# A decoder step on one core: earlier transfers for the pooling buffers, a held background convolution, a separate key loop and other filler places

## The chip, the core and the metric

The kernel runs on one core of a Trainium2 chip. Its time is the device time of one execution in microseconds (us); the lower, the better. TensorE (PE in the rows) multiplies, VectorE (DVE) and ScalarE (ACT) do everything elementwise, GpSimd (POOL) and SyncE (SP) mostly issue transfers.

## What is computed

One step of a two-layer decoder trunk, over 1024 prompt positions and 8 samples of 8 positions (1088 columns in all), with 1024 features in float32. Layer 0 is a mixer of two branches, layer 1 a pooling mixer; each is followed by a SwiGLU network.

```python
def _conformer_conv(u, buf, w_dw, b_dw, g, b):          # layer 0, branch 1
    a, gate = jnp.split(u, 2, axis=-1)
    glu = a * jax.nn.sigmoid(gate)
    ext = jnp.concatenate([buf.astype(glu.dtype), glu], axis=1)
    y = lax.conv_general_dilated(ext, ...)              # 31 taps, each channel by itself
    y = y + b_dw.astype(y.dtype)
    y = jax.nn.silu(_layernorm(y, g, b))                # mean and variance over 512 channels
    return y, ext[:, -(CONV_WIDTH - 1):]
...
def _pool_mixer(xn, buf, pos0, w_pool, pool_scale):     # layer 1
    ext = jnp.concatenate([buf.astype(xn.dtype), xn], axis=1)
    ...                                                 # per group: trailing mean over 2, 4, 8 or 16, minus the token
    y = jnp.einsum('btgc,gcd->btgd', d, w_pool).reshape(n, t, D_MODEL)
    return y * pool_scale.astype(y.dtype), ext[:, -POOL_BUF:]
```

Branch 2 of layer 0 is sliding-window attention with sinks. `buf` of the pooling mixer is zero for the prompt; for the samples it is the input `state_pool` (15 earlier positions of each sample), which the kernel holds in HBM as `spool`.

## The kernel before

Features lie on the 128 partitions, positions along the columns. The 1088 columns are cut into NC = 4 chunks of TW = 272, two chunks to a half h (h = 0 and 1); the samples are the last 64 columns of chunk 3. Every float32 product is made of three matmuls of split operands (`mm3`, L311), whose high and low parts are made by `split` (L323): ScalarE writes the high part, VectorE the low one. A weight tile is transferred on SP's queue (`Weights.raw`, L127) and split in the same way (`whi`, `wlo`). The sums over channels for the norms are matmuls with a constant matrix (`ones_d`, `ones_v`, `ones_h`) in plain float32.

TensorE executes in the order of the program. On the other engines a scheduler lays down a fixed order when the kernel is built, in which a ready instruction can be put ahead of an earlier one that is not ready; each engine then executes its own list strictly in that order. Work that belongs to a matmul's result is put in `later` and written by `flush` (L300) at the end of the next `mm3` or step. The convolution's 31 taps per channel tile (`conv_taps`, L445; 480 columns for h = 1, 544 for h = 0) and the samples' convolution (`conv_sample`, L460) are background work of VectorE: they stand in `bg` (h = 0 and samples) and `bg1` (h = 1), and `pump` (L306) writes some of them whenever its estimate of VectorE's time is behind that of TensorE. `bg` goes ahead of `bg1`.

The stages that the change touches, in order of time:

- Input projection (L602 to L643). `Glu(0)` and the key weights go through one loop over the chunks: `gl.a(c)`, `gl.g(c)`, then `measure(c + 1)` (L413: squares of the next chunk, eight float32 matmuls, reciprocal root, and, by `later`, that chunk's split operands), then `heads('k', u, c)`.
- Attention (L645 to L812). 16 steps of `turn` (transposes), `scores` and `values_out`. The 16 parts of `Glu(2)` and `Glu(3)` are fillers: four go ahead of the loop, and every step i except 15 calls `filler()`, so that the twelve that are left go into steps 0 to 11. `filler` without a part only calls `flush`.
- Output projection (L873 to L909). First the four attention tiles, then the four convolution tiles; `while bg` at o == 1 empties `bg`, and `Layer(0)` (L473) makes the norm over channels: mean matmuls, `center`, variance matmuls, reciprocal root, `out`. Mean and variance are eight matmuls each.
- `half_pass` (L1093), four times: a SwiGLU network for one half, in NP = 11 stages j of `gate_up` (seven steps of 24 matmuls) and `down`. In the first one, `while bg1` and `Layer(1)` stand at j == 9. In the second and third, `pool_in` and `pool_mix` at j = 2, 4, 6 and 8 (`POOL_AT`) make one of the four pooling groups for half 0 and half 1. The samples are in half 1: for chunk 3, `pool_in` takes a tile `es` from the seven rotating buffers `t` (`wide`, L271), fills it from `spool` on POOL's queue and writes the new state out on the same queue:

```python
            if c == NC - 1:
                es = wide()[:, :DEC * (PB + DEC)].rearrange("p (b t) -> p b t", b=DEC)
                G.dma_start(out=es[:, :, 0:PB], in_=I['spool'][:, kt])
                V.scalar_tensor_tensor(es[:, :, PB:], src[:, n:]..., gain, r[:, n:]..., ALU.mult, ALU.mult)
                s, inv = sums(es, g, DEC)
                ...
                G.dma_start(out=O['pool_s'][:, kt], in_=es[:, :, DEC:])
```

  This happens twice per group (k = 0 and 1), with 60 KB each. The tile `ca1` is a single buffer, in which the taps of h = 1 and then the reciprocal root of `Layer(1)` lie.
- `emit_y` (L1075) writes the result out on SP's queue, two row tiles at a time.

Of the kernel before, what the change touches and what calls it, by code (L numbers as in the profile page):

```python
# [18 lines left out]
P = 128  # L19
# [229 lines left out]
def _body(ctx, tc, I, O):  # L249
# [21 lines left out]
    def wide():  # L271

        return tp.tile([P, PB + 2 * TW + 1], F32, tag="t", bufs=NT, name="t")

    def both():
        return pair_of(wide())
# [18 lines left out]
    def bank2():  # L295
        return pp.tile([P, 2, 512], F32, tag="pp", name="pp")[:, :, :TW]

    later, bg, bg1 = [], deque(), deque()

    def flush():  # L300
        todo, later[:] = list(later), []
        for f in todo:
            f()
        pump()

    def pump(slack=0.0):  # L306
        while (bg or bg1) and V.t < T.t + slack:
            (bg or bg1).popleft()()
        V.t = max(V.t, T.t - LAG)

# [162 lines left out]
    class Layer:  # L473
# [3 lines left out]
        def __init__(self, h):  # L477
            self.h = h
            e = [E[h][:, ct, 0:2 * TW] for ct in range(CT)]
            e2 = [pair_of(x) for x in e]  # L480
            mb = bank2()
            for ct in range(CT):
                for k in range(2):
                    T.matmul(out=mb[:, k], lhsT=ones_v, rhs=e2[ct][:, k], start=ct == 0, stop=ct == CT - 1)

            def center():
                sqs = []
                for ct in range(CT):
                    V.scalar_tensor_tensor(e2[ct], mb, 2.0, e2[ct], ALU.mult, ALU.add)
                    sq = both()  # L490
                    S.activation(sq, e2[ct], AF.Square)
                    sqs.append(sq)
                later.append(lambda: var(sqs))

            def var(sqs):
                vb = bank2()
                for ct in range(CT):
                    for k in range(2):
                        T.matmul(out=vb[:, k], lhsT=ones_v, rhs=sqs[ct][:, k], start=ct == 0, stop=ct == CT - 1)
                r = pair_of((cvp, tp)[h].tile([P, 2 * TW], F32, tag=f"ca{h}", bufs=1, name="ca"))  # L500
                rsqrt_of(r, vb, 1, lambda: out(r))

            def out(r):
                for ct in range(CT):
                    V.tensor_tensor(e2[ct], e2[ct], r, ALU.mult)
                    S.activation(e[ct], e[ct], AF.Silu, scale=pcol('cn_g', ct), bias=pcol('cn_b', ct))
            later.append(center)
# [84 lines left out]
    def heads(name, u, c):  # L592
        b = project(u, c)
        o = C0[c]
        if name == 'k':
            head_norm(b, c, [(HALF[kv], kz[HALF[kv], kv, o:o + TW]) for kv in range(2)], pcol('kg'))
        elif name == 'v':
            values(b, c)
        else:
            head_norm(b, c, [(slice(0, P), Q[c // 2][:, int(name[1]), c % 2 * TW:c % 2 * TW + TW])], pcol('qg'))  # L600
# [3 lines left out]
    for c in range(NC):  # L604
        gl.a(c)
        if c == 0:
            for kt in range(KT):
                feed(x0[0][:, kt, :], kt == 0, 0)
        gl.g(c)
        if c + 1 < NC:  # L610
            measure(c + 1)
        if c == 0:
            w0.pop(0)()
        heads('k', u, c)
    flush()
    x0_pool.__exit__(None, None, None)
# [183 lines left out]
            split(y.pair(p), Q[h][:, 2 * p:2 * p + 2, :])  # L800

    for i in range(16):
        if i != 15:
            filler()
        if i == 13:
            Y = Act(xp, 0)
            attn_split(0, Y)
        turn(i)
        if i + 2 < 16:
            scores(i + 2)  # L810
        values_out(i)
# [29 lines left out]
    def operands(h, goff):  # L841
# [28 lines left out]
                job(diff, 'T3', 'B22', 'B12', 'B12'), job(cut, 'B22', 12), job(cut, 'T3', 10), job(cut, 'T4', 14)]  # L870
        return x, deque(first), deque(rest)

    ua = W.take(4)  # L873
    for o in range(KT):
        b = bank2()
# [138 lines left out]
    def sums(e, g, n):  # L1014
# [6 lines left out]
            cur, wd = nx, 2 * wd  # L1021
        return cur, 1.0 / wd

    def pool_in(c, g):

        x = slot(xp, c % 2, 4)
        r, n = RS[c // 2][:, c % 2], PC[c]
        for k in range(2):
            kt = 2 * g + k
            gain, src = pcol('norm_mix', KT + kt), pair_of(rt(c // 2, kt))[:, c % 2]  # L1030
            e, d = ext[k], tmp()
            S.activation(e[:, 0:PB], halo[:, kt, :], AF.Copy)
            V.scalar_tensor_tensor(e[:, PB:PB + n], src[:, :n], gain, r[:, :n], ALU.mult, ALU.mult)
            S.activation(halo[:, kt, :], e[:, n:n + PB], AF.Copy)
            s, inv = wide(), 0.5 / 2 ** g
            w = 2 * 2 ** g
            if g == 0:
                V.tensor_tensor(s[:, PB:PB + n], e[:, PB:PB + n], e[:, PB - 1:PB - 1 + n], ALU.add)
            else:
                V.tensor_tensor_scan(s[:, 0:PB + n], e[:, 0:PB + n], hist[k][:, 16 - w:16 - w + PB + n], 0.0,  # L1040
                                     ALU.add, ALU.subtract)
            V.scalar_tensor_tensor(d[:, 0:n], s[:, PB:PB + n], inv, e[:, PB:PB + n], ALU.mult, ALU.subtract)
            if c == 0:
                t = hp.tile([P, 16], F32, tag="s16", bufs=2, name="s16")
                V.tensor_tensor(t, s[:, PB:PB + 16], pcol('rcnt', 16 * g, 16), ALU.mult)
                V.tensor_tensor(d[:, 0:16], t, e[:, PB:PB + 16], ALU.subtract)
            if c == NC - 1:
                es = wide()[:, :DEC * (PB + DEC)].rearrange("p (b t) -> p b t", b=DEC)
                G.dma_start(out=es[:, :, 0:PB], in_=I['spool'][:, kt])
                V.scalar_tensor_tensor(es[:, :, PB:], src[:, n:].rearrange("p (b t) -> p b t", b=DEC), gain,  # L1050
                                       r[:, n:].rearrange("p (b t) -> p b t", b=DEC), ALU.mult, ALU.mult)
                s, inv = sums(es, g, DEC)
                V.scalar_tensor_tensor(d[:, n:].rearrange("p (b t) -> p b t", b=DEC), s[:, :, PB:], inv,
                                       es[:, :, PB:], ALU.mult, ALU.subtract)
                G.dma_start(out=O['pool_s'][:, kt], in_=es[:, :, DEC:])
            split((x[:, k, :], x[:, 2 + k, :]), d)
        if c == NC - 1 and g == 3:
            G.dma_start(out=O['pool_p'], in_=halo)
        return x
# [13 lines left out]
            feed_res(half, oo)  # L1073

    def emit_y(h, o):  # L1075
        if o % 2 == 1:
            nc.sync.dma_start(out=O[f'y{h}'][:, o - 1:o + 1, :], in_=res[h][o // 4][:, o % 4 - 1:o % 4 + 1])

    POOL_AT = {2: 0, 4: 1, 6: 2, 8: 3}
# [13 lines left out]
    def half_pass(l, half, x, pooled, after, following, mixed=False):  # L1093
# [4 lines left out]
        for j in range(NP):  # L1098
            if pooled is not None and j == 1:
                finish(pooled)  # L1100
                flush()
            if pooled is not None and j in POOL_AT:
                ds = [pool_in(c, POOL_AT[j]) for c in (2 * pooled, 2 * pooled + 1)]
            if mixed and j == NP - 2:
# [30 lines left out]
            steps.popleft()()  # L1135
        return nx if following is not None else None

    plan(0, False, True)
    plan(0, True)
    plan(1, True)  # L1140
# [142 lines left out]
```

## Time and profile before

| | before |
|---|---|
| median of 3 runs | 2000.65 us (1999.78 to 2005.07) |
| the profiled execution | 2002.05 us, of which the span is 2000.3 us |
| TensorE busy | 1909.4 us, 95% of the span |
| VectorE busy | 1670.3 us, 84% |
| ScalarE busy | 946.5 us, 47% |
| granted TensorE clock, mean | 0.981 of full speed |

The profile is of one execution. The span runs from the first instruction to the last, and 1.75 us lie outside of it. Busy shares are means over stages that differ much; so the profile is read by stage, and a stage's idle time of TensorE together with its granted clock tells what could be had there. One step of matmuls with 272 columns can be seen at either of the two clock levels, and where the granted clock is 0.5 it takes twice the time.

### The profile page before, as it was taken

The numbers are of one execution on the slowest core, as the hardware profiler recorded it, in microseconds if no ns is written. First come the engines' busy times: TensorE is split into PE (matmuls) and PEld (weight loads), VectorE is DVE, ScalarE is ACT, GpSimd is POOL, SyncE is SP. The second block draws the span as 40 slices with busy tenths as digits, with TensorE's granted clock in tenths as the row PEclk, the third lists the DMA queues.
The fourth block names the chain that finished last, engine by engine and source line by source line (L and its number), as shares of the span: only waits on it lengthen the run. The fifth ranks groups of instructions, "written<-read, shape, count | busy, mean of one in ns | idle before, by whom it ended". The sixth has DMA issues, their size and how long they took to land.

```text
span 2000.3 us, 34797 instructions
## 1 busy us (share of the span) xinstructions
PE 1909.4 (95%) x14461; PEld 1854.2 (93%) x14461; DVE 1670.3 (84%) x2587; ACT 946.5 (47%) x1613; POOL 32.6 (2%) x47
## 2 busy tenths in 40 slices
PE   7999989799999999899999999899898999999999
PEld 6898658799999999799999998898898999999998
DVE  6999999998777776998898899787787898878784
ACT  7534775544343553554544446444443544343432
POOL 1100000000000000000000000000000000000000
PEclk9999999899999999999999999999998999999999
DMA  5220103132323241132322223323223323232321
GB/s 191 89 61 1 35 9 124 43 103 88 106 85 106 85 161 54 43 132 75 117 74 98 99 85 104 76 77 114 85 76 85 118 96 127 84 107 84 107 85 67
DMA packets 52191, 177.75 MB, mean 89 GB/s; under 512 B 5968, under 2 KB 10672, under 8 KB 51488
## 3 DMA queue, kind: packets, MB, share of 16 engines
q1 hardware_dynamic: 50672, 172.12, 25.7%
q0 software_dynamic: 1360, 3.40, 0.8%
q8 instruction: 113, 1.85, 0.4%
q14 instruction: 46, 0.38, 0.1%
HBM read 169.74 MB, written 6.74 MB: 88 GB/s over the span
## 4 chain that ended last, share of the span: by engine, by line
PE 78%; DVE 14%; ACT 4%; DMA 2%; issue 2%; POOL 0%; DVEq 0%; ACTq 0%; POOLq 0%
PE pp L111 68%; PE ps L111 10%; DVE x L111 3%; DVE wlo L111 2%; DVE t L111 2%; DVE res L111 2%; DVE ca L111 2%; DMA raw<-w 1%; DVE raw L111 1%; ACT whi L111 1%; DMA t<-spool 1%; ACT P L111 1%; ACT t L111 1%; DVE ss L111 1%; ACT x L111 0%
## 5 line engine op out<-in xcount | busy, mean ns | idle before, releaser
L111 PE MATMUL pp<-x,whi 128*128 128x272 f32 x5568 | 1076.1, 292 | 38.7 <-ACT t L111 26.4
L111 PEld LDWEIGHTS pp<-x,whi 128*128 128x128 f32 x5568 | 890.0, 191 | 44.2 <-ACT t L111 28.8
L111 PE MATMUL pp<-x,wlo 128*128 128x272 f32 x2784 | 813.4, 292 | 3.6 <-DVE wlo L111 3.6
L111 ACT ACTIVATE whi<-raw 128x1024 fp32r<-128x1024 f32 (+1 forms) x390 | 407.3, 1048 | 538.4 <-PE pp L111 362.2
L111 DVE TENSOR_TENSOR wlo<-raw,whi 128x1024 fp32r<-128x1024 f32 (+1 forms) x386 | 465.0, 1209 | 118.1 <-ACT whi L111 117.7
L111 PEld LDWEIGHTS pp<-x,wlo 128*128 128x128 f32 x2784 | 532.0, 191 | 4.7 <-DVE wlo L111 4.7
L111 PE MATMUL pp<-hh,whi 128*128 128x272 f32 x1408 | 408.2, 290 | 6.6 <-DVE res L111 4.3
L111 PE MATMUL pp<-hh,wlo 128*128 128x272 f32 x1408 | 407.2, 289 | 0.0
L111 PE MATMUL pp<-hl,whi 128*128 128x272 f32 x1408 | 405.5, 288 | 0.0
L111 PEld LDWEIGHTS pp<-hh,whi 128*128 128x128 f32 x1408 | 265.1, 188 | 8.5 <-DVE res L111 4.4
L111 PEld LDWEIGHTS pp<-hl,whi 128*128 128x128 f32 x1408 | 265.3, 188 | 0.0
L111 PEld LDWEIGHTS pp<-hh,wlo 128*128 128x128 f32 x1408 | 264.8, 188 | 0.0
L111 PE MATMUL ps<-x,whi 128*128 128x272 f32 x896 | 184.3, 302 | 12.9 <-ACT whi L111 7.9
L111 DVE TENSOR_TENSOR g<-pp,g 128x544 f32<-128x544 f32 x184 | 129.6, 717 | 44.9 <-PE pp L111 44.2
L111 PEld LDWEIGHTS ps<-x,whi 128*128 128x128 f32 x896 | 147.1, 194 | 21.4 <-ACT whi L111 7.9
L111 DVE TENSOR_TENSOR t<-pp,t 128x544 f32<-128x544 f32 (+1 forms) x176 | 113.8, 647 | 43.8 <-PE pp L111 40.3
L111 DVE TENSOR_TENSOR res<-pp,res 128x544 f32<-128x544 f32 (+1 forms) x200 | 135.4, 693 | 13.4 <-PE pp L111 12.8
L111 PE MATMUL ps<-x,wlo 128*128 128x272 f32 x448 | 131.8, 294 | 0.4 <-DVE wlo L111 0.4
L111 ACT ACTIVATE hh<-t 128x272 fp32r<-128x272 f32 x176 | 74.7, 426 | 107.4 <-DVE t L111 106.7
L111 ACT ACTIVATE t<-t 128x272 f32<-128x272 f32 x170 | 72.1, 427 | 92.1 <-DVE t L111 91.6
L111 DVE TENSOR_TENSOR raw<-raw 128x1024 f32<-128x1024 f32 x88 | 107.0, 1216 | 0.0
L111 ACT ACTIVATE t<-pp 128x544 f32<-128x544 f32 (+1 forms) x176 | 97.2, 553 | 15.5 <-PE pp L111 13.7
(164 smaller groups left out, 1546.8 us busy)
## 6 DMA issues: line engine op xcount, KB each, us to landing
raw<-w SPq DMA_DIRECT2D x294, 512.0 KB, 3.3
x<-x SPq DMA_DIRECT2D x16, 272.0 KB, 8.6
res<-x SPq DMA_DIRECT2D x2, 1088.0 KB, 6.3
g<-x SPq DMA_DIRECT2D x2, 1088.0 KB, 5.7
o_y<-res SPq DMA_DIRECT2D x4, 544.0 KB, 2.7
o_y<-g SPq DMA_DIRECT2D x4, 544.0 KB, 2.7
raw<-w SPq DMA_DIRECT2D x8, 256.0 KB, 4.4
P<-bias SPq DMA_DIRECT2D x2, 512.0 KB, 4.5
```

What stands on the lines that cost most here:

```text
L111: return f(*a, **k)
```

## The change

Seven edits:

1. Pooling. The samples' buffer `es` no longer comes out of `t`. A new function `history(g)` takes one tile for both k out of the single buffer `ca1` and issues both `spool` transfers on POOL's queue; it is called in the third `half_pass` at j = 1, 3, 5 and 7, one stage ahead of the group's `pool_in`.
2. `Layer(1)` adds its four channel tiles on VectorE (three additions for the mean, three for the variance) and then needs two matmuls in place of eight, twice. `Layer(0)` stays.
3. `bg1` is held from the start of the output projection to the first `half_pass`: `pump` then writes `bg` alone.
4. The key projection leaves the chunk loop and gets a loop of its own behind it; `measure(c + 2)` takes the place of `measure(c + 1)`, and chunk 0 does `measure(1)`, a `flush` and `measure(2)`.
5. The fillers skip steps 2, 6, 10 and 15 and so reach to step 14.
6. With 5, the last gate result of `Glu(3)` is still in `later` when the output projection starts, so that its samples' convolution and its taps are put in the queues there.
7. `emit_y` writes the last four row tiles of half 1 one at a time.

```diff
-    later, bg, bg1 = [], deque(), deque()
+    later, bg, bg1, hold = [], deque(), deque(), []
...
-        while (bg or bg1) and V.t < T.t + slack:
+        while (bg or bg1 and not hold) and V.t < T.t + slack:
...
-            mb = bank2()
-            for ct in range(CT):
-                for k in range(2):
-                    T.matmul(out=mb[:, k], lhsT=ones_v, rhs=e2[ct][:, k], start=ct == 0, stop=ct == CT - 1)
+            def mean(src):
+                if h:
+                    a = both()
+                    V.tensor_tensor(a, src[0], src[1], ALU.add)
+                    for x in src[2:]:
+                        V.tensor_tensor(a, a, x, ALU.add)
+                    src = [a]
+                b = bank2()
+                for i, x in enumerate(src):
+                    for k in range(2):
+                        T.matmul(out=b[:, k], lhsT=ones_v, rhs=x[:, k], start=i == 0, stop=i == len(src) - 1)
+                return b
+            mb = mean(e2)
...
-                vb = bank2()
-                for ct in range(CT):
-                    for k in range(2):
-                        T.matmul(out=vb[:, k], lhsT=ones_v, rhs=sqs[ct][:, k], start=ct == 0, stop=ct == CT - 1)
+                vb = mean(sqs)
...
         gl.g(c)
-        if c + 1 < NC:
-            measure(c + 1)
+        if c == 0:
+            measure(1)
+            flush()
+        if c + 2 < NC:
+            measure(c + 2)
         if c == 0:
             w0.pop(0)()
+    for c in range(NC):
         heads('k', u, c)
...
     for i in range(16):
-        if i != 15:
+        if i not in (2, 6, 10, 15):
             filler()
...
+    hold.append(True)
     ua = W.take(4)
...
+    es2 = {}
+
+    def history(g):
+
+        t = tp.tile([P, 2 * TW], F32, tag="ca1", bufs=1, name="es")[:, :2 * DEC * (PB + DEC)]
+        es2[g] = t.rearrange("p (k b t) -> p k b t", k=2, b=DEC)
+        for k in range(2):
+            G.dma_start(out=es2[g][:, k, :, 0:PB], in_=I['spool'][:, 2 * g + k])
...
-                es = wide()[:, :DEC * (PB + DEC)].rearrange("p (b t) -> p b t", b=DEC)
-                G.dma_start(out=es[:, :, 0:PB], in_=I['spool'][:, kt])
+                es = es2[g][:, k]
...
     def emit_y(h, o):
-        if o % 2 == 1:
+        if h and o > 3:
+            nc.sync.dma_start(out=O[f'y{h}'][:, o, :], in_=rt(h, o))
+        elif o % 2 == 1:
...
+            if pooled == 1 and j + 1 in POOL_AT:
+                history(POOL_AT[j + 1])
...
+    hold.clear()
     plan(0, False, True)
```

## Rows read from the trace of the kernel before

**Rows 1.** Page, head and part 1: engine, busy us, share, instructions.

```profile
span 2000.3 us, 34797 instructions
...
PE 1909.4 (95%) x14461; PEld 1854.2 (93%) x14461; DVE 1670.3 (84%) x2587; ACT 946.5 (47%) x1613; POOL 32.6 (2%) x47
```

**Rows 2.** Windows by stage; its first line names the columns.

```profile
core 0: us, PE busy (x) PEld busy (x) DVE busy (x) ACT busy (x) POOL busy (x), PEclk, DMA share, GB/s
0.00:40.00 40.00, 29.62 (x170) 26.80 (x171) 20.57 (x51) 27.23 (x58) 6.24 (x13) 0.96 0.70 238
40.00:75.00 35.00, 28.94 (x178) 25.56 (x177) 34.30 (x71) 24.50 (x48) 1.40 (x3) 0.95 0.17 57
...
278.80:304.50 25.70, 18.89 (x74) 8.87 (x72) 24.11 (x67) 19.25 (x55) 0.00 (x0) 0.80 0.10 26
304.50:342.80 38.30, 35.55 (x232) 33.03 (x232) 36.26 (x56) 18.88 (x23) 0.00 (x0) 0.96 0.35 127
342.80:392.00 49.20, 34.32 (x238) 32.83 (x238) 48.60 (x84) 24.24 (x39) 0.00 (x0) 0.90 0.16 54
392.00:475.00 83.00, 83.00 (x646) 83.00 (x647) 80.58 (x105) 39.22 (x57) 0.00 (x0) 0.98 0.27 91
475.00:675.00 200.00, 200.00 (x1589) 200.00 (x1588) 153.87 (x195) 83.46 (x121) 0.00 (x0) 1.00 0.28 97
...
1234.00:1581.00 347.00, 324.14 (x2481) 321.87 (x2480) 279.18 (x417) 149.82 (x246) 14.85 (x17) 0.97 0.31 92
```

**Rows 3.** Waits, 1250 to 1560: waiter <- awaited: us in total, times, longest.

```profile
DVE t L111 <- DMA t<-spool: 22.3, 4, 6.6
PE pp L111 <- ACT t L111: 22.2, 8, 5.0
```

**Rows 4.** Timeline of POOL: start, us, instruction, [idle before <- who ended it].

```profile
1269.88 0.89 POOL L1055 DMA_DIRECT2D o_pool_s<-t  x1 [9.12 <-DVE t L111]
1276.46 0.90 POOL L1049 DMA_DIRECT2D t<-spool  x1 [5.70 <-issue]
```

**Rows 5.** Timeline of DVE behind the second transfer of the first group.

```profile
1281.12 0.22 DVE L111 TENSOR_TENSOR t<-t 128x64 f32<-128x64 f32 x1 [5.59 <-DMA t<-spool]
```

**Rows 6.** DMA issues: tiles, queue, count, KB each, median us to landing.

```profile
o_y<-g SPq DMA_DIRECT2D x4, 544.0 KB, 2.7
...
o_pool_s<-t POOLq DMA_DIRECT2D x8, 60.0 KB, 5.8
```

**Rows 7.** Timeline of PE: the `finish` matmuls at j = 1 and 9, passes two and three.

```profile
845.93 1.08 PE L111 MATMUL pp<-ss,ones_d 128*128 128x272 f32 x4
...
1158.80 1.08 PE L111 MATMUL pp<-ss,ones_d 128*128 128x272 f32 x4
...
1233.78 1.08 PE L111 MATMUL pp<-ss,ones_d 128*128 128x272 f32 x4
...
1579.97 1.08 PE L111 MATMUL pp<-ss,ones_d 128*128 128x272 f32 x4
```

**Rows 8.** Timeline of PE: mean matmuls of `Layer(1)`, and the next step's first.

```profile
677.79 3.83 PE L111 MATMUL pp<-g,ones_v 128*128 128x272 f32 x16
...
681.25 0.49 PE L111 MATMUL pp<-x,whi 128*128 128x272 f32 x1
```

**Rows 9.** Waits of PE, 304.5 to 392.

```profile
PE pp L111 <- DVE ss L111: 7.4, 2, 5.9
PE pp L111 <- ACT x L111: 3.7, 1, 3.7
```

**Rows 10.** Groups by form: h = 1 taps, 299 to 342.8, then 342.8 to 392.

```profile
L111 DVE SCALAR_TENSOR_TENSOR ca<-g,prm,ca 128x480 f32<-128x480 f32 x26 | 18.6, 716 | 0.6
...
L111 DVE SCALAR_TENSOR_TENSOR ca<-g,prm,ca 128x480 f32<-128x480 f32 x9 | 6.4, 712 | 0.1
```

**Rows 11.** Windows of attention steps: one without its projection, then step 12.

```profile
261.40:265.10 3.70, 3.70 (x23) 1.94 (x21) 3.63 (x14) 3.03 (x7) 0.00 (x0) 1.00 0.00 0
278.80:287.00 8.20, 6.14 (x22) 2.54 (x20) 8.20 (x25) 5.46 (x17) 0.00 (x0) 0.79 0.11 17
```

## The prediction

> **What bounds the kernel now.** The page first: TensorE is busy for 95% of the span and VectorE for 84% [rows 1], so there are some 91 us without a matmul (2000.3 - 1909.4), and nothing else is near its limit. Where they lie is read from the windows by stage [rows 2]. From 392 to 675 TensorE is busy all the time at nearly full clock. The rest is in two places. In the front, from 40 to 392, VectorE is as full as TensorE or fuller: 34.3 of 35 us, 24.1 of 25.7, 48.6 of 49.2, while TensorE idles for 6.1, 6.8, 2.8 and 14.9 us in the four windows shown, with the clock down to 0.80 and 0.90 in two of them. In the third pass, 1234 to 1581, TensorE idles for 22.9 us though VectorE has 68 us to spare: that is a wait, and no lack of an engine. The waits name it: VectorE stood still four times for 22.3 us until a `spool` transfer had landed, and TensorE then for 22.2 us behind ScalarE [rows 3].
>
> **Pooling, the largest part.** The second `spool` transfer of the first group is issued at 1276.46, 6.6 us after the new state of the first buffer went out at 1269.88 [rows 4]; such a write lands after 5.8 us at the median [rows 6]. So the second buffer waited for the first to be written out. VectorE reached the addition that needs it, waited 5.59 us [rows 5], and everything behind it on its list waited too: the gate results that free TensorE's banks. The price of all this can be had without guessing. The second and the third pass do the same matmuls between their two `finish` points and differ in the samples' part. The second takes 1158.80 - 845.93 = 312.9 us, the third 1579.97 - 1233.78 = 346.2 us [rows 7]. The difference of 33.3 us holds the waits, and the half clock after them (0.97 over 347 us is about 10 us at full speed). The change issues both transfers one stage earlier: a stage is 312.9 / 8 = 39 us here, a transfer some 5 us. They stand on POOL's queue behind the writes of the group before, which were issued in the stage before, and POOL has 14.9 us of work in 347; the buffer `ca1` is free once those writes have landed. What remains is the samples' arithmetic, on VectorE in both kernels and covered by its 68 us. I take -31 us; bounds are -33.3 (the third pass becomes the second) and -22 (the waits go, the slow clock stays).
>
> **Layer(1).** Eight float32 matmuls took from 677.79 to 681.25, 3.46 us or 0.43 each [rows 8]. Twelve of sixteen go: -5.2 us on a TensorE that is never idle there. Six additions of 544 columns come to VectorE, which has 46 us free between 475 and 675 [rows 2]. They could make TensorE wait: the first three need only the finished taps and can be done ahead; the second three come after the squares, with two steps of matmuls, some 6 us, as cover. I take -5; bounds -5.2 and -1 (all six, at 0.7 us each, seen in full).
>
> **Held taps.** Between 299 and 392 VectorE did 35 taps of h = 1 at about 0.7 us, 18.6 + 6.4 = 25 us [rows 10]. The first ten or so had been written before the hold starts and stay. Of the waits in this stretch, 7.4 us are for the squares of the new residual and 3.7 for the next operands [rows 9]: both stand at the end of VectorE's list, of which taps are a part. The nine taps after 342.8 stand directly in front of the longest waits: -6 us; and of the 4.9 us that 0.90 of clock costs over 49.2 us [rows 2], two go with them. In 304.5 to 342.8 TensorE idles for only 2.8 us; nothing is taken there, since edit 6 brings other work to that place: the samples' convolution of the last tile (about 5 us) and what is left of its taps for h = 0, on which `Layer(0)` waits. I take -8; bounds -18 (nearly all 14.9 + 4.9 us) and 0 (what is put there costs as much). The held taps run in the first pass, where VectorE has 2.4 us free up to 475 and 46 us up to 675 [rows 2]; they need some 26. `pump` writes them only as fast as its account of TensorE allows, and 392 to 475 shows VectorE at 97% with TensorE never idle, so I cost them at nothing; the rival below is what they cost if that cover fails.
>
> **Fillers.** A step without its projection is 3.7 us of work, but step 12 took 8.2 us [rows 11]: the chain from the scores over VectorE and ScalarE to the next transposes is longer than two short steps. The last four steps took 25.7 us for about 11.2 us of work (two at 3.7, two without scores at an estimated half), so 14.5 us are the most that spreading can win. Against it: steps 2, 6, 10 and 15 become short, and at step 12's loss of 4.5 us each they would cost 18 us, 3.5 more than now. A short step between long ones has the neighbour's 3 us of projection to wait in, so I put them nearer the good end, but VectorE's list up to the output projection stays as long as it was and was 94% full. I take -3; bounds -14.5 and +3.5.
>
> **Key loop.** From 40 to 75 TensorE idles for 6.1 us and loses 1.7 us at half clock (5% of 35) [rows 2], which I put down to the operands of chunks 2 and 3: the loop needs them one key projection after their measurement. They now come a chunk earlier, partly ahead of 40 us, where VectorE is busy for 20.6 of 40 us. In exchange `measure(2)` stands ahead of chunk 1's projection and could hold TensorE up once while its squares are made, by about what its eight matmuls take, 3.5 us [rows 8]. I take -4.5; bounds -7.8 and +3.5.
>
> **Tail.** The last write of 544 KB takes 2.7 us [rows 6]; half of it is at best 1.3 us less and I take -0.3. The two more issues on SP's queue have nothing behind them.
>
> **Sum.** 31 + 5 + 8 + 3 + 4.5 + 0.3 = 51.8 us off the profiled execution's 2002.05 us gives 1950.3. That execution lies 1.4 us above the median, so the forecast is 1949 us.
>
> **One rule weighed.** Rows 2 say that in the front TensorE waits while VectorE is 94 to 99% full. The Trainium skill (Perfetto Trace Analysis, Identifying Performance Opportunities) says that improving kernels generally means improving the most-contended engine, regime by regime. In the front that is VectorE, and by that rule edits 4 and 5, which take nothing off it, give nothing: the forecast would be 1956.5. Rival 1 goes further in the same direction.
>
> **Rivals.**
> 1. *The front gives nothing.* VectorE bounds it, the late taps of the last tile and the samples' convolution take the place of the held taps in front of `Layer(0)`, and the short steps cost what the long ones win. For it: the shares in rows 2. Against it: the 25 us of taps do leave. Then 2000.65 - 31 - 5 = 1964.6.
> 2. *The prefetch does not come early.* If the transfers wait for `ca1` or behind POOL's writes until the stage itself, the third pass stays at 346 us and the rest is won: 1980. Against it: 39 us a stage, 5.8 us a write.
> 3. *Slower: the held taps bind the first pass.* Place: 392 to 475, where 26 us of held taps meet VectorE's 2.4 us. If they stand on its list ahead of weight halves, TensorE waits. The point from which it decides is about 12 us of taps in a row, since four weight tiles are ready ahead and one lasts 3 us (24 matmuls). Price: 26 - 2 = 24 us of waiting, and the clock of rows 2's worst stage, 0.80, over 107 us, 21 us; with the last tile's other taps, which are on that list already, pushed back as well (31 less the nine of rows 10 and some four ahead of them, 12 us), it is 57 us: 2006. Against it: the pacing.
> 4. *Better:* the front's idle time goes nearly whole, 20 us more: 1929.
>
> **How the numbers follow.** Forecast 0.71, rival 1 0.17, rival 2 0.05, rival 3 0.03, rival 4 0.04. The forecast's own range is 1936 to 1960, from the bounds above taken half way together; 8 in 10 is reached with rival 1 and its spread: 1935 to 1971. About 0.3%, 6 us, is what a measurement of this kernel can tell from no change. Faster by more than that: all but rival 3 and a sliver of rival 2, 0.96; within it 0.02; slower 0.02, since part of rival 3 falls within it.
>
> **What would show it.** Third pass: `finish` to `finish` 313 to 316 us, no VectorE wait for `spool`, clock 1.00. `Layer(1)`: two float32 matmuls in each of its two places, 0.9 us, with no wait before them. Taps of 480 columns gone between 311 and 392 and present up to some 600, with TensorE still never idle in the first pass. The wait for the squares before the second `finish` of the output projection down from 5.9 us to about 2. Attention steps 12 to 14 at 5 to 7 us each, with small waits at 2, 6 and 10. Wrong would be: a wait for `spool` that stays; TensorE idle between 392 and 475; a wait of TensorE on the channel means of `Layer(0)`.

## The result, and the profile after

| | before | after |
|---|---|---|
| median | 2000.22 us (1997.04 to 2005.07, 4 runs) | 1965.97 us (1963.84 to 1972.5, 4 runs) |
| ratio | | 0.9832, 95% interval 0.9802 to 0.9863 |
| the profiled execution | 2002.05 us, span 2000.3 us | 1965.52 us, span 1963.7 us |

The change saves 34.3 us. The forecast was 1949 with a range of 1935 to 1971: the range held the time, but the time is 17 us above the forecast, outside the forecast's own 1936 to 1960, and stands beside rival 1 (1964.6, "the front gives nothing"), for which the range had been widened. Of e11 below, the execution that was profiled took 3702.73 us, against 1953.2 to 1961.8 for its other four, and is left out of its figures.

The page of the changed kernel, head and part 1, as in [rows 1]:

```profile
span 1963.7 us, 34755 instructions
...
PE 1887.9 (96%) x14437; PEld 1835.1 (93%) x14437; DVE 1670.9 (85%) x2593; ACT 940.5 (48%) x1609; POOL 32.6 (2%) x47
```

VectorE does as much as before (1670.3), only in other places. Where the time went is again read from the windows by stage, with the columns of [rows 2]; the limits are moved to the same events:

```profile
0.00:40.00 40.00, 27.48 (x150) 23.68 (x151) 24.84 (x62) 31.71 (x71) 6.23 (x13) 1.00 0.70 238
40.00:75.00 35.00, 33.27 (x255) 32.28 (x254) 33.23 (x68) 20.79 (x40) 4.17 (x7) 1.00 0.30 94
...
168.60:296.90 128.30, 115.29 (x690) 79.40 (x690) 120.58 (x353) 93.67 (x288) 2.92 (x4) 0.97 0.08 24
296.90:338.00 41.10, 37.16 (x231) 34.29 (x231) 38.81 (x61) 18.48 (x22) 0.00 (x0) 0.90 0.32 117
338.00:386.00 48.00, 34.57 (x239) 33.40 (x240) 46.20 (x81) 22.80 (x37) 0.00 (x0) 0.87 0.14 47
386.00:475.00 89.00, 89.00 (x690) 89.00 (x691) 85.64 (x112) 41.94 (x60) 0.00 (x0) 0.97 0.29 95
475.00:672.00 197.00, 197.00 (x1565) 197.00 (x1565) 155.47 (x197) 81.85 (x119) 0.00 (x0) 1.00 0.28 94
...
1226.40:1545.00 318.60, 314.76 (x2483) 313.26 (x2482) 278.33 (x418) 150.18 (x248) 13.05 (x15) 1.00 0.32 100
```

Two things are to be seen. The third pass, the last line, is now TensorE's own: 3.8 us idle in place of 22.9, clock 1.00 in place of 0.97. The output projection, 296.9 to 386, is no shorter (88.9 us from its first matmul to the first one of the SwiGLU network, 86.7 before): VectorE is busy for 85 of 89 us, TensorE idle for 17.4 us, the clock at 0.90 and 0.87. That is where 8 us had been forecast.

The third pass, by its two `finish` points, as in [rows 7], takes 1544.05 - 1226.37 = 317.7 us (before 346.2):

```profile
1226.37 1.08 PE L111 MATMUL pp<-ss,ones_d 128*128 128x272 f32 x4
...
1544.05 1.08 PE L111 MATMUL pp<-ss,ones_d 128*128 128x272 f32 x4
```

No wait of VectorE for a transfer of `spool` is left between 1240 and 1530, and of TensorE's 22.2 us [rows 3] there remain two kinds:

```profile
PE pp L111 <- DVE t L111: 2.1, 1, 2.1
PE pp L111 <- ACT t L111: 1.7, 2, 1.5
```

POOL's timeline shows how ([rows 4] is the same place before). Both writes of group 0 go out; then both transfers of group 1 are issued in a row, one landing after the other, and VectorE's additions over them start at 1335, some 60 us later (the last line below is VectorE's):

```profile
1241.43 0.90 POOL L1074 DMA_DIRECT2D o_pool_s<-es  x1 [543.52 <-DVE es L111]
1247.36 0.89 POOL L1074 DMA_DIRECT2D o_pool_s<-es  x1 [5.03 <-DVE S L111]
1270.08 0.89 POOL L1042 DMA_DIRECT2D es<-spool  x1 [21.83 <-DVE t L111]
1275.24 0.89 POOL L1042 DMA_DIRECT2D es<-spool  x1 [4.27 <-DMA es<-spool]
...
1335.01 0.23 DVE L111 TENSOR_TENSOR t<-es 128x80 f32<-128x80 f32 x1
```

`Layer(1)` ([rows 8] before) has two matmuls in each of its two places, one for each half of the bank (two records each), but the second pair waits:

```profile
672.30 1.08 PE L111 MATMUL pp<-t,ones_v 128*128 128x272 f32 x4
...
682.13 1.15 PE L111 MATMUL pp<-t,ones_v 128*128 128x272 f32 x4 [2.69 <-DVE t L111]
```

The waits of TensorE between 297 and 386, against [rows 9]: the longest, for the squares before the second `finish`, is 5.8 us (before 5.9), and a new one, for the operands of the convolution's half, has come in at 338:

```profile
PE pp L111 <- DVE ss L111: 6.6, 2, 5.8
PE pp L111 <- DVE x L111: 5.4, 3, 3.1
PE pp L111 <- ACT x L111: 4.7, 1, 4.7
```

And the taps of h = 1 that were to be held, by form, from 296.9 to 338 and from 338 to 386:

```profile
L111 DVE SCALAR_TENSOR_TENSOR ca<-g,prm,ca 128x480 f32<-128x480 f32 x16 | 11.4, 715 | 0.3
...
L111 DVE SCALAR_TENSOR_TENSOR ca<-g,prm,ca 128x480 f32<-128x480 f32 x7 | 5.0, 717 | 0.1
```

[rows 10] has 26 and 9 for the kernel before, but its first window begins at 299, in the attention. From the first matmul of the output projection, from 305.2 to 343, it is this line:

```profile
L111 DVE SCALAR_TENSOR_TENSOR ca<-g,prm,ca 128x480 f32<-128x480 f32 x20 | 14.3, 715 | 0.5
```

So sixteen such taps stand where twenty stood, and seven where nine stood; five taps of h = 0 and a second sum for the samples (edit 6) have come in beside them, and VectorE's work in the stretch is the same (85.0 us, before 84.2). That was to be explained first.

### The profile page after: what moved, and what is told of

The parts are those of the page before. It is cut to its first block, busy times and chain, and to the rows that moved or that the text cites. A ratio compares the mean times of both kernels' runs of the same rounds, so it can differ in the third digit from the quotient of the medians.

```text
span 1963.7 us, 34755 instructions
## 1 busy us (share of the span) xinstructions
PE 1887.9 (96%) x14437; PEld 1835.1 (93%) x14437; DVE 1670.9 (85%) x2593; ACT 940.5 (48%) x1609; POOL 32.6 (2%) x47
## 4 chain that ended last, share of the span: by engine, by line
PE 84%; DVE 10%; ACT 3%; DMA 2%; issue 1%; SPq 0%; ACTq 0%; DVEq 0%
PE pp L111 74%; PE ps L111 10%; DVE x L111 3%; DVE wlo L111 2%; DVE res L111 1%; DVE ca L111 1%; ACT P L111 1%; DMA raw<-w 1%; ACT t L111 1%; DVE g L111 1%; DVE raw L111 1%; DVE t L111 1%; DVE ss L111 1%; ACT x L111 0%; DMA x<-x 0%
## 5 line engine op out<-in xcount | busy, mean ns | idle before, releaser
L111 PE MATMUL ps<-x,whi 128*128 128x272 f32 x896 | 178.5, 297 | 7.0 <-ACT whi L111 7.0
L111 ACT ACTIVATE hh<-t 128x272 fp32r<-128x272 f32 x176 | 74.6, 426 | 108.8 <-DVE t L111 107.9
```

What stands on the lines that cost most here:

```text
L111: return f(*a, **k)
```

## What the instruction lists say without a run

The kernel can be built with and without an edit, and the list of every engine compared, instruction for instruction. Three answers came from that alone.

- **The hold changes nothing.** Without `hold.append(True)` all five lists are the same as with it, entry for entry. The kernel before with the hold added has the lists of the kernel before. And yet the hold acts on `pump`: without it 14 taps are written during the output projection, with it none. So for these taps the scheduler does not care where in the program they are written. It puts a ready instruction ahead, and they are ready: the taps of the third channel tile are all written behind `hold.clear()`, and in the trace they run from 250.9 us on, before the output projection starts.
- **The stage ahead changes nothing.** With `history(g)` called at the group's own stage and not one ahead, the lists are the same too. What edit 1 brings is the tile of its own, from which readiness follows.
- **The fillers and the key loop do change the lists**, since TensorE's order is that of the program.

## Experiments

Stages are read from the starts of matmuls: the first score matmul of the samples, the first of the output projection, the second `finish`, the next `finish` (end of the first pass), and the third pass from `finish` to `finish`. A `finish` is the norm whose sums of squares are the matmuls `pp<-ss,ones_d` above. All of it in us; e11 has no trace that can be read by stage:

| kernel | to the scores | attention | to 2nd `finish` | to next `finish` | third pass | ratio to before |
|---|---|---|---|---|---|---|
| before | 175.6 | 129.6 | 71.3 | 411.6 | 346.2 | 1 |
| after | 168.6 | 128.3 | 73.5 | 410.8 | 317.7 | 0.9832 (0.9802 to 0.9863) |
| after, again (e9) | 171.2 | 128.3 | 74.6 | 410.6 | 315.2 | 0.9810 (0.9795 to 0.9825) |
| e1 pooling alone | 175.2 | 128.7 | 72.1 | 411.4 | 314.8 | 0.9841 (0.9821 to 0.9862) |
| e2 old key loop | 173.4 | 128.4 | 74.7 | 410.7 | 315.9 | 0.9838 (0.9819 to 0.9856) |
| e3 old fillers | 168.4 | 130.1 | 72.2 | 410.3 | 315.5 | 0.9808 (0.9792 to 0.9824) |
| e4 old `Layer(1)` | 167.9 | 130.1 | 74.8 | 412.2 | 315.7 | 0.9830 (0.9809 to 0.9850) |
| e5 taps really held | 169.0 | 124.5 | 69.1 | 408.0 | 315.3 | 0.9753 (0.9738 to 0.9767) |
| e6 and a third tile | 175.4 | 122.4 | 69.4 | 411.5 | 315.9 | 0.9752 (0.9735 to 0.9768) |
| e7 buffer alone | 175.1 | 129.5 | 71.9 | 411.4 | 329.0 | 0.9917 (0.9897 to 0.9936) |
| e8 adds for the mean only | 170.9 | 127.5 | 73.2 | 409.3 | 314.4 | one run |
| e10 before, taps held | 173.4 | 127.7 | 69.8 | 409.7 | 343.4 | 0.9948 (0.9934 to 0.9962) |
| e12 e5, e8, old fillers | 172.9 | 129.4 | 69.5 | 406.9 | 314.7 | 0.9766 (0.9750 to 0.9783) |

e1 to e4 ran on one chip, e5 to e8 on a second, e9 to e12 on a third; the kernel before took 2004.5, 2002.45 and 2004.9 us there. The two rows of the changed kernel show how far one profile of a stage can be trusted: 2.6 us apart up to the scores, 2.5 in the third pass, at the same program.

### e1: edit 1 alone

```diff
-                es = wide()[:, :DEC * (PB + DEC)].rearrange("p (b t) -> p b t", b=DEC)
-                G.dma_start(out=es[:, :, 0:PB], in_=I['spool'][:, kt])
+                es = es2[g][:, k]
```

with `history` as in the change. 

> The kernel before with edit 1 alone. Theory 1 (the transfers that came too late were nearly the whole gain, and the stage shows it): the third pass goes from 346.2 to about 317.7 us from finish to finish, all other stages stay as in the kernel before, total 2000.2 - 28.5 = 1971.7 us. Theory 2 (the prediction's sum: the other six edits are worth 21 us, and some of the pooling's gain is given back elsewhere): the total comes out at 1980 or more, because the change as a whole has 1966.

Measured: 1973.3 us against 2004.5, 31.2 us less; third pass 1551.08 - 1236.32 = 314.8 us, the other stages as before. Theory 2 falls: this one edit is worth 31 of the 34 us (of 38 in e9). The other six together are worth 0.9841 - 0.9810 = 0.31% of 2003, 6 us by e9's ratio and 2 by the first one, where the forecast had 20.8.

### e7: a buffer of its own, without the rest of edit 1

```diff
-                es = wide()[:, :DEC * (PB + DEC)].rearrange("p (b t) -> p b t", b=DEC)
+                es = tp.tile([P, 2 * TW], F32, tag="ca1", bufs=1, name="es")[:, :DEC * (PB + DEC)].rearrange(...)
```

> The kernel before with the samples' pooling buffer taken from the single buffer ca1, one channel tile at a time, and no early transfers. Theory 1 (the rotation of the seven buffers t was the trouble, any buffer of its own does): third pass 315 to 320 us from finish to finish, as with edit 1. Theory 2 (the trouble is the row write of the first tile, transfer in of the second, both in front of VectorE's next addition; edit 1 helps because one tile holds both): VectorE still waits about 5 us for a transfer in each group, third pass 335 to 350 us.

Measured: third pass 1563.16 - 1234.21 = 329.0 us, between the two theories, and 16 us in the total. VectorE's and TensorE's waits between 1250 and 1530:

```profile
DVE es L111 <- DMA o_pool_s<-es: 6.1, 2, 3.3
...
PE pp L111 <- ACT t L111: 12.0, 6, 4.4
```

Both theories hold a half. Out of the rotation of seven buffers the pass wins 17 us. But with one tile for both k, the second may only be filled when the first has been written out; VectorE waits for that write, and TensorE for 12.0 us in place of the 22.2 in [rows 3] and the 1.8 in e1. Room for both at once is the other 14 us.

### e2: the key projection back in the loop

```diff
-        if c == 0:
-            measure(1)
-            flush()
-        if c + 2 < NC:
-            measure(c + 2)
+        if c + 1 < NC:
+            measure(c + 1)
...
-    for c in range(NC):
         heads('k', u, c)
```

> The changed kernel with the key projection back in the chunk loop (edit 4 undone). Theory 1 (what the key loop wins before 75 us is kept, since TensorE was waiting there for operands of its own): the attention starts some 6 us later, near 175, the first matmul of the first SwiGLU pass at about 392 in place of 386, total about 1972. Theory 2 (VectorE bounds everything up to that matmul, so a gain ahead of it is lost again before it): the attention starts later, but the pass starts at 387 to 388, total 1967.

Measured: the scores start at 173.4 and the first SwiGLU matmul at 391.9, as theory 1 has it (385.8 and 389.5 in the changed kernel); from the scores to the second `finish` it takes 203.1 us, as in the changed kernel (201.8 and 202.9). A gain ahead of a VectorE-bound stage is not lost in it here, since VectorE's list came earlier too. The ratio against e9's is 0.28% more, 5.6 us, though the intervals meet; against the first ratio of the changed kernel it is 1 us. Over all runs the scores start at 170.5 (eight kernels with the new loop, 167.9 to 175.4) and at 174.5 (five with the old one): 4.0 us.

The 4 us are not idle time. Up to the scores, before and after:

```profile
0.00:175.60 175.60, 157.73 (x1109) 150.04 (x1110) 154.17 (x317) 92.18 (x189) 14.83 (x26) 0.98 0.30 97
...
0.00:168.60 168.60, 152.76 (x1109) 146.52 (x1110) 150.66 (x312) 86.12 (x184) 14.80 (x26) 1.00 0.31 101
```

For the same matmuls TensorE is busy for 157.7 to 158.2 us in the five kernels with the old loop, at a clock of 0.98, and for 152.6 to 154.9 us in seven of the eight with the new one, at 0.99 to 1.00 (in e6 159.2, at 0.96). Its idle time up to there is 16.6 and 16.4 us in the mean. So what the new loop wins shows in the clock, and not in fewer waits.

### e3: the fillers as before

```diff
-        if i not in (2, 6, 10, 15):
+        if i != 15:
             filler()
```

> The changed kernel with the fillers in steps 0 to 11 again (edits 5 and 6 undone). Theory 1 (VectorE, busy for 94% of the attention and of the output projection, sets their length, so the place of the projections does not matter): attention and output projection together last 216 to 218 us as in both kernels, total within 2 us of the changed kernel's 1966. Theory 2 (the prediction: TensorE's waits in steps 12 to 15 are latency, and long and short steps side by side hide it): together they last 220 us or more, total 1969 to 1970. Theory 3 (edit 6, which brings the last tile's convolution into the output projection, costs what 5 wins): attention 130, output projection 86 to 87, sum unchanged.

Measured: 0.9808 against e9's 0.9810. From the scores to the first SwiGLU matmul it takes 386.2 - 168.4 = 217.8 us (changed kernel 217.2, and 218.3 in e9; before 216.3). The sum is that of theories 1 and 3, and the split is near theory 3's: attention 130.1, output projection 87.6 (128.3 and 88.9 in the changed kernel, 128.3 and 90.0 in e9). TensorE's wait of 3.1 us at 338 in the changed kernel, which e9 has too, is not there. The waits have only moved: in the changed kernel TensorE waits 3.2 us at 291.8, in step 15, and the last steps run at a granted clock of 0.84, by the window of these steps:

```profile
281.00:296.90 15.90, 11.78 (x67) 7.17 (x65) 15.26 (x36) 11.21 (x28) 1.45 (x2) 0.84 0.16 42
```

The same steps in e5, below, where TensorE's longest wait there is 0.7 us:

```profile
281.00:293.50 12.50, 10.40 (x68) 6.36 (x66) 11.99 (x28) 11.05 (x28) 0.91 (x2) 1.00 0.13 42
```

In both windows VectorE has hardly a free moment (15.3 of 15.9 us, 12.0 of 12.5). Attention and output projection up to the second `finish` together: 202.7 us at the mean of after, e2, e4, e8 and e9 (200.7 to 204.9), 201.4 with the old fillers (before, e1, e3, e7; 200.7 to 202.4). By parts, the attention is 1.0 us shorter in the mean with the new fillers (128.5 and 129.5), and the output projection up to the second `finish` 2.3 us longer (73.2 to 74.8, against 71.3 to 72.2): so by the stages edit 6 costs there at least what edit 5 wins, though e3 undoes both and cannot part them. Spreading did not win 3 us; it is within a microsecond or so of nothing, if not a loss.

### e4 and e8: `Layer(1)`

e4:

```diff
-                if h:
+                if False:
                     a = both()
```

> The changed kernel with both sums over channels of Layer(1) on TensorE again (edit 2 undone). Theory 1 (the additions for the variance stand on VectorE's list behind weight halves, and TensorE waits 2.70 and 0.95 us there; the net gain is about 1.6 us): the eight mean matmuls and the eight variance matmuls take 3.5 us each again, the two waits are gone, total 1967 to 1968. Theory 2 (the prediction: 5 us): total 1971.

e8, with the additions for the mean alone:

```diff
-            def mean(src):
-                if h:
+            def mean(src, add=False):
+                if add:
...
-            mb = mean(e2)
+            mb = mean(e2, h)
```

> The changed kernel with the additions on VectorE for the mean alone; the variance is summed by eight matmuls again. Theory 1 (only the additions behind the squares make TensorE wait): no wait before the variance matmuls, which take 3.5 us; from the second finish to the end of the first pass about 1 us less than with both (410.8). Theory 2 (the squares themselves come late and the additions cost little): a wait of 1 to 2 us stays, and the stretch gets 1 us longer.

Measured: e4's ratio, 0.9830 against 0.9810, can't tell the theories apart. The stage can: with eight matmuls each it is 411.4, 411.6 and 412.2 us (e1, before, e4), with the additions 410.3 to 410.8 (after, e2, e3, e9), 1.1 us less, and without them no wait of TensorE stands between 670 and 700. In e8 the variance's matmuls follow without a wait:

```profile
680.30 3.83 PE L111 MATMUL pp<-t,ones_v 128*128 128x272 f32 x16
```

The squares themselves are in time; it is the three additions behind them that TensorE waits for, 2.69 us, and 0.95 us more one step on. So 5.2 us of matmuls less, and 3.6 us of waiting more. The stage of e8 is 409.3 us, the lowest of those without held taps, by a single run; e12 below has the same edit, and its stage is 1.1 us shorter than e5's (406.9 and 408.0). In the time of e11 the same edit shows no difference.

### e5: a hold that cannot be passed

The taps are made to need something that does not exist earlier: a bias that ScalarE computes from the last operand of the first pass, with scale 0.

```diff
-                V.tensor_scalar(a[0], e[:, k:k + n], wk, pcol('b_dw', ct), ALU.mult, ALU.add)
+                V.tensor_scalar(a[0], e[:, k:k + n], wk, late[:, ct:ct + 1] if h and ct in (2, 3) else pcol('b_dw', ct),
+                                ALU.mult, ALU.add)
...
-                bg1.extend(conv_taps(ct, 1))
+                (bg2 if ct in (2, 3) else bg1).extend(conv_taps(ct, 1))
...
-    hold.clear()
+    for ct in (2, 3):
+        S.activation(late[:, ct:ct + 1], r32(X['T4'][1][:, 0, 0:1]), AF.Identity, scale=0.0, bias=pcol('b_dw', ct))
+    bg1.extend(bg2)
```

> The changed kernel, with a hold that cannot be passed: the first tap of h = 1 of channel tiles 2 and 3 takes its bias from a small tile that ScalarE writes after the last operand of the first SwiGLU pass, so that those 62 taps cannot run before it. 24 taps (some 17 us of VectorE) leave the output projection and must run in the first pass. Theory 1 (VectorE, busy for 85 of 89 us there, is what TensorE waits for): the wait for the squares before the second finish falls from 5.8 to 2 us or less, the stretch from the first output-projection matmul to the first SwiGLU matmul goes from 88.9 to about 80 us, total about 8 us less than the changed kernel. Theory 2 (TensorE waits there for a chain from engine to engine, into whose gaps the scheduler puts the taps): that stretch gets shorter by 3 us at most. Theory 3 (the prediction's third rival, with taps now really held): from the second finish to the one after the first pass it takes over 415 us in place of 410.8.

Measured: 1953.3 us against 2002.45, and against the changed kernel's ratio 0.57% less, 11 us. Its windows from the scores on:

```profile
169.00:293.50 124.50, 113.58 (x691) 79.22 (x691) 115.11 (x339) 93.13 (x288) 2.38 (x4) 0.99 0.07 23
293.50:332.00 38.50, 35.77 (x235) 33.19 (x235) 25.89 (x44) 17.66 (x21) 0.55 (x1) 0.96 0.37 117
332.00:376.50 44.50, 32.64 (x235) 31.37 (x235) 41.36 (x73) 23.34 (x37) 0.00 (x0) 0.92 0.22 72
376.50:475.00 98.50, 98.50 (x771) 98.50 (x772) 95.93 (x125) 47.74 (x70) 0.00 (x0) 0.98 0.28 97
475.00:662.00 187.00, 187.00 (x1488) 186.96 (x1488) 169.07 (x223) 77.59 (x114) 0.00 (x0) 1.00 0.27 91
```

39 tap instructions have moved behind the front, 25 from the output projection and 14 from the attention, and VectorE does 333 us of work up to the first SwiGLU matmul (150.7 + 115.1 + 25.9 + 41.4) in place of 356. The attention is 3.8 us shorter, the output projection 83.0 in place of 88.9 us: between theories 1 and 2. What theory 1 said of the longest wait failed:

```profile
PE pp L111 <- DVE ss L111: 6.1, 2, 5.1
...
PE pp L111 <- ACT x L111: 3.1, 1, 3.1
```

5.1 us in place of 5.8, with no tap near it. That wait is for VectorE too, but for its own work of the place, which fills 41.4 of the 44.5 us: weight halves, residuals, operands. So the taps were a part of what fills VectorE there, and not what that wait is for. Theory 3 falls. The held taps run from 398 to 571, TensorE is busy for 98.50 of 98.50 and 187.00 of 187.00 us, and VectorE has 20 us left there.

### e6: a third tile held

The same with `ct in (1, 2, 3)`. 

> As e5, with channel tile 1 held as well: 31 more taps, 22 us of VectorE, leave the attention. Theory 1 (VectorE bounds the attention): from the first score matmul to the output projection it takes 120 us or less in place of 128 to 130. Theory 2 (the chain from scores over VectorE and ScalarE to the transposes sets the attention's length): 126 us or more. Theory 3 (93 held taps, 67 us, are more than VectorE has free before they are needed): TensorE waits between 386 and 680, and the total is not below that of e5.

Measured: 0.9752, the same as e5. The profiled execution took 1960.8 us, 7 more than the median of four (1953.9), so its stages are less typical than e5's. Three windows: up to the scores, the attention, and the end of the first pass:

```profile
0.00:175.40 175.40, 159.25 (x1108) 150.78 (x1108) 150.80 (x312) 86.23 (x184) 14.84 (x26) 0.96 0.29 97
175.40:297.80 122.40, 115.23 (x691) 81.37 (x691) 100.46 (x317) 93.07 (x287) 2.92 (x4) 0.95 0.08 25
...
475.00:669.00 194.00, 191.81 (x1525) 191.62 (x1525) 191.17 (x260) 81.39 (x119) 0.00 (x0) 1.00 0.27 89
```

15 us of VectorE less than in e5 make the attention 2.1 us shorter: with VectorE at 82% it is no longer VectorE that bounds it, and theory 1 (120 us) fails as theory 2 (126 us) does. Theory 3 begins to hold: VectorE is busy for 191.2 of 194 us, and TensorE waits 2.2 us for the mean of `Layer(1)`. What the third tile wins in the attention (2.1 us) is given back in the first pass (411.5 us in place of 408.0), so two tiles are about as much as that pass takes at no cost.

### e9 to e12: the changed kernel again, and combinations

e9 is the changed kernel itself. 

> The changed kernel once more, beside the next three on one chip, so that its ratio to the kernel before can be set against theirs. Theory 1: 0.983 again, and e3 with the fillers of before (0.9808) is no slower or a little faster. Theory 2 (the fillers' new places do help, and e3's ratio is chance of its chip): 0.980 or less.

Measured: 0.9810, with 1966.9 us. Theory 1 named 0.983 and theory 2 0.980 or less; it lies between, and e3 is equal to it.

e10 is the kernel before with the gate of e5 and nothing else. 

> The kernel before with only the hold of e5 (62 taps of h = 1 that cannot run ahead of the first pass). Theory 1 (a hold that works pays by itself): the stretch from the attention to the first SwiGLU matmul gets 8 to 13 us shorter, as in e5, total 1988 to 1994 of some 2002. Theory 2 (it pays only with edits 5 and 6, since in the kernel before the last tile's own taps are ready early and the output projection is less crowded): 1997 or more.

Measured: 1995.2 us against 2004.9, 0.52% less, 10 us: it pays by itself. From the scores to the first SwiGLU matmul it takes 211.3 us, 5.0 less than before (1.9 in the attention, 3.1 in the output projection, from which all 30 taps have gone), which is less than theory 1 said of the stretch; the rest of the 10 us lies in small differences of stages that one profile can't resolve.

e11 is e5 with e8's edit. 

> e5 with the additions of Layer(1) for the mean alone, as in e8. Theory 1 (gains in different stages add up): 1 to 2 us less than e5's ratio of 0.9753, about 0.9745. Theory 2 (the six additional matmuls cost what the wait did): 0.9753.

Measured: 1954.1 us, 0.9755 (0.9736 to 0.9775), e5's ratio. Only the time is read. The additions for the variance cost too little to be told by the time.

e12 is e11 with e3's edit. 

> e11 with the fillers in steps 0 to 11 as in the kernel before. Theory 1 (their place does not matter where VectorE sets the length of the attention, and edit 6 brings work into the output projection): equal to e11 or 1 to 3 us faster. Theory 2 (with 24 taps gone VectorE has room, and then TensorE's waits in the last steps are what is left: spreading pays): 3 to 6 us slower than e11.

Measured: 1958.1 us, 4.0 us more than e11 by the medians, which is theory 2, but only 2.2 us by the ratios, whose intervals overlap. The stages point the same way: attention and output projection up to the second `finish` take 198.9 us, as in e10 with the same fillers (197.4), and 193.6 in e5 and 191.8 in e6 with the new ones. With the taps held, the attention's window has VectorE at 90% and TensorE waiting all the same:

```profile
172.90:302.25 129.35, 114.53 (x690) 80.25 (x691) 115.84 (x347) 92.86 (x287) 2.91 (x4) 0.96 0.08 23
```

So spreading the fillers is worth nothing while VectorE is full (e3), and some 4 to 5 us when it is not (e5 against e12). That the two edits need each other is what the stages of these four kernels point to, one profile each; the times alone don't settle it.

e5, e6, e11 and e12 beat both kernels; e5 is the simplest, 2.5% below the kernel before.

## Why the prediction was right and wrong

| term | forecast | measured | from |
|---|---|---|---|
| pooling | -31 | -31 | e1; third pass 346.2 to 315.2 in e9 (317.7 in the first profile) |
| `Layer(1)` | -5 | -1 | stage of e4 and others; 5.2 less and 3.6 of waits |
| held taps | -8 | 0 | the lists are the same with and without the hold |
| fillers | -3 | +1, not told from 0 | e3; stages: -1.0 attention, +2.3 output projection |
| key loop | -4.5 | -4 | start of the scores; e2 |
| tail | -0.3 | not told apart | |
| sum | -51.8 | -35 | the change: -34.3, in e9 -38.0 |

That the range held the time owes something to luck: the pooling and the key loop came as forecast in size, the held taps, the fillers and most of `Layer(1)` did not come, and the range reached down to their loss only because rival 1 names the same sum for other reasons.

**Pooling: right, in size and in price.** Taking the second pass as the measure of the third gave the term to within what a stage can be read. One part of the step was wrong without harm: the transfers do not come a stage ahead because `history` is called there, since the lists are the same without that. They come when the tile is free, behind the group before, which is some 60 us ahead of use.

**Held taps: the step failed at its root.** It costed a change of the written order as a change of VectorE's order. That the scheduler can put a ready instruction ahead of an earlier one had been noted in the description of the kernel; it was not applied to the hold. "The nine taps after 342.8" were to give 6 us, and two more of the clock, and they did not go. Nor had "the first ten or so" been written before the hold starts: of the third channel tile none had. The mechanism behind it was right in part: where the taps truly leave, 10 us (e10) and 11 us (e5) are won, but only 3.1 and 5.9 of them in the output projection, the place that was priced at 8; another 1.9 and 3.8 lie in the attention, where the forecast had nothing. One step within it was wrong: the wait of 5.9 us before the second `finish` was put down to the taps in front of it, and it stays at 5.1 without them.

**Fillers: the sign was not safe.** Rival 1's ground was that the short steps cost what the long ones win. By the stages the attention does win, 1.0 us, and the cost of 2.3 us is in the output projection, where edit 6 brings work that the sum had at nothing. The bounds (-14.5 to +3.5) held; the choice of -3 "nearer the good end" had no row for it.

**`Layer(1)`: mis-sized.** The cover counted for the second three additions, two steps of matmuls, is too short by 2.7 us. The lower bound of -1 is what came.

**Key loop: right in size, not in where it comes from.** TensorE idles for 1.7 us between 40 and 75 (before 6.1; in e9 4.2) and for 12.5 up to 40 (before 10.4), where `measure(2)` stands early; 3.5 us had been allowed for that. But the idle time up to the scores is the same in the mean with either loop (e2). The forecast drew its term from 6.1 us of idle time and only 1.7 of the clock; what came is TensorE's busy time, at a higher clock. That the sizes agree is luck.

**Rivals.** Rival 1 had the time for part of its reason. It held that VectorE bounds the front, and that fits the output projection and the end of the attention. The work that it names did come into the output projection, with edit 6. But the key loop's gain came through, and the held taps had not left: the hold does nothing. Rival 2 falls with the timeline of POOL. Rival 3 is refuted for two tiles by e5, and its limit is seen in e6. TensorE is never idle between 392 and 475 in any of these. Rival 4 falls: no kernel here comes near 1929.

**The rule weighed.** The Trainium skill (Perfetto Trace Analysis, Identifying Performance Opportunities) names the most-contended engine as the thing to improve. The runs agree for the fillers, which take nothing off VectorE and gave nothing, and for e5; they disagree for the key loop, which gave its 4 us. The Trainium skill (Perfetto Trace Analysis, Optimization Strategy) also says that, where the most-contended engine changes over time, interleaving the regimes may help. The runs agree; that is e5: 23 us of VectorE's work moved from where it is full to where TensorE is, and 11 us won.

## What to carry to other kernels

Where a scheduler orders by readiness, holding back the writing of an instruction holds back nothing: give it an operand that is made late, and compare the engine's lists with and without the edit before any time is forecast for it. A buffer that takes part in a rotation or serves two transfers in turn ties a load to the write before it; room for both parts at once is worth more than an earlier call. And where one engine is full, an edit on another may pay only after the full one has been relieved (the fillers; the key loop paid without that), so price them together. A term whose size comes out is not yet a term whose reason is right: look for the gain in the quantity that the forecast drew it from.

## What was not expected of the chip

The same program, profiled twice, differs by 2.6 us up to the scores: the wait ahead of a key norm at about 60 us is 0.5 us in one and 2.9 in the other. In e6, whose profiled execution was a long one, the same stage took 4 to 7 us more, with the granted clock at 0.96 over it where after and e5 have 1.00, though its program up to there brings TensorE the same work. So terms of 5 us or less, four of the forecast's six, cannot be read from one profile of each kernel; the stage's mean over several kernels that share the code did it here. What decides whether the clock falls in such a stage was not found. Nor does a step at the lower level take quite twice the time: in the changed kernel a matmul of 272 columns starts 0.227 us after the one before it at a granted clock of 0.50 (302 to 304), and 0.127 us at 1.00 (500 to 520), 1.8 times as much.
